# RWKV time mixing: six batches transposed on TensorE instead of by DMA transposes out of DRAM

## The chip, the cores and the metric

The kernel runs on one core of a Trainium2 chip. The metric is the device time of one execution in microseconds (us). Each kernel is run several times; one further execution is taken with the hardware profiler, and its durations are those quoted below. A core has TensorE (PE: matmuls and transposes; its weight loads are shown as PEld), VectorE (DVE), ScalarE (ACT), GpSimd (POOL), SyncE (SP, which here only issues transfers) and 16 DMA engines.

## The reference

x has 16 batches of 2048 tokens with 256 channels, float32. What counts for the output:

```python
x_prev[:, 1:, :] = x[:, :-1, :]          # the token before; zeros for the first
xv = x * time_mix_v + x_prev * (1 - time_mix_v)
xr = x * time_mix_r + x_prev * (1 - time_mix_r)
v = xv @ value_weight                    # 256 x 256
r = xr @ receptance_weight
out = (sigmoid(r) * v) @ output_weight
```

The key path of the reference does not reach its output, and the kernel leaves it out.

## The kernel before

**Units.** The 32768 tokens are cut into 64 units of 512 tokens (TU), four to a batch (UB). Channels lie on the partitions: 256 channels are two halves of 128 (KO), so x must be transposed before it can be mixed and multiplied. A batch is loaded by one software DMA from GpSimd (load, line 158 or 162), which also casts float32 to bf16.

**Two ways to a transposed x.** Batches 0 to 9 are loaded into SBUF tiles x_bf (four buffers), 16 tokens to a partition. For each of their units transposes() issues 8 transposes of 128x128 on TensorE into a PSUM tile ps_t (line 272), and ScalarE copies ps_t to xt_both (line 289). A slot of 128 columns then holds every 16th token, so the previous token of a slot is mostly the slot before it; one slot of a batch is a copy of another, shifted by one column (wrap_slots, line 557). Batches 10 to 15 (STAGED and up) are loaded into a DRAM tile x_natural as bf16 instead, in two groups of three, with 16 rows of zeros ahead of each batch (zero_rows, line 142). Two DMA transposes issued from SP (by_dma, line 254), in the passes of units 27 and 39 (T_AT), put a whole group into xt_both with tokens in their natural order. They wait for the loads of their group, and three later loads (STAGE_AT) wait for the first of them. Stores whose units are named in FIRST and WAITING are held back and issued around the DMA transposes.

**One unit.** With the mixing folded into the weights, a projection's input is c * previous + current. The product is made for one half of the channels on VectorE (line 354) and for the other on GpSimd (line 364), over two units at once from unit 10 on; VectorE adds the current tokens (line 376). project() (line 384) does four matmuls of 512 columns for r into psum_r and four for v into psum_v; ScalarE makes the sigmoid (line 658); VectorE multiplies it with psum_v into z_sb (line 697). output() multiplies z with the output weight in eight matmuls of 256 columns (line 416), ScalarE copies the result to an output tile (line 471), and SP stores it (line 437), two units to a store. Output tiles come from opool (seven buffers) and, late in the run, also from the x_bf buffers that are no longer needed.

**Order.** The order of each engine's instructions is the order in which the program writes them. The loop at the end of the kernel writes one pass for each unit g: r of unit g; the transposes of unit g + 6 (advance; LOOK is 6), with the loads that LOADS ties to them; v of unit g; z; the output of the unit before. In the free stage, from FREE = 34 on, when no transposes are left, ScalarE makes VectorE's product for v (scale_act, line 638), and the output runs two units behind instead of one.

Of the kernel before, what the change touches and what calls it, by code (L numbers as in the profile page):

```python
# [15 lines left out]
def kernel(  # L16
# [25 lines left out]
    nc = tc.nc  # L42
# [13 lines left out]
    STAGED = 10  # L56
    BYDMA = NU - STAGED * UB
    CROSS = NU - BYDMA - LOOK
    FREE = CROSS
    LATE_O = CROSS - 2  # L60
    T_AT = {27: 10, 39: 13}
    FIRST = {19: 27, 21: 27, 27: 39}
    WAITING = {23: 27, 25: 27, 29: 39, 31: 39, 33: 39, 35: 39}
    ZEROS_AT = 12
    SINGLE = NU - 6
    STAGED_PAIRS = range(STAGED, B - 1)
    STAGE_AT = {33: 13, 34: 14, 35: 15}
    GROUPS = [(2, 3), (4, 5, 6), (7, 8, 9), (10, 11, 12), (13, 14, 15)]
    HALVED = (12, 15)
    PAD = 16  # L70
    SPARE = 9 * UB // 2
# [7 lines left out]
    LOADS = {  # L79
        (1, 1): (3,),  # L80
        (1, 2): (4,),
        (2, 0): (5,),
        (3, 0): (6,),
        (4, 0): (7,),
        (5, 0): (8, 10),
        (6, 0): (9,),
        (7, 0): (11,),
        (7, 1): (12,),
    }
# [3 lines left out]
    dpool = ctx.enter_context(tc.tile_pool(name="dpool", bufs=2, space=bass.MemoryType.DRAM))  # L93
# [14 lines left out]
    kept = {}  # L108
    firsts = {}
    x_bf = {}  # L110
    x_both = {}
    loads = {}
# [20 lines left out]
    def new_staged(group):  # L133

        x_both[group[0]] = dpool.tile([len(group), PAD + S, D], BF16, name="x_natural")
        for k in range(len(group)):
            x_bf[group[0] + k] = x_both[group[0]][k, PAD:].rearrange("(p j) d -> p j d", p=P)
        return [(group[0], k) for k in range(len(group))]

    def zero_rows(b, k):  # L140
        rows = zeros[k * PAD : (k + 1) * PAD].rearrange("p (o c) -> p o c", o=1)
        nc.gpsimd.dma_start(
            out=x_both[b][k, :PAD].rearrange("p (h c) -> p h c", c=P),
            in_=rows.to_broadcast([PAD, KO, P]),
        )

    def load(b):
        if b < STAGED:
            x_bf[b] = xpool.tile([P, J, D], BF16, name="x_bf")
        if b < BYUNIT:  # L150
            for e in range(UB):
                nc.gpsimd.dma_start(  # L152
                    out=x_bf[b][:, e * UJ : (e + 1) * UJ, :], in_=unit_rows(x, b, e)[:, 0]
                )
            return
        if b in HALVED:
            return [
                nc.gpsimd.dma_start(out=x_bf[b][:, j : j + J // 2], in_=rows(b)[:, j : j + J // 2])
                for j in (0, J // 2)
            ]  # L160
        run = 8192 if b < LONG else 16384
        return nc.gpsimd.dma_start(out=x_bf[b], in_=rows(b), max_dma_last_dim=run)  # L162
# [47 lines left out]
    def new_xt(b):  # L210
        if b >= BYUNIT:
            for group in GROUPS:
                if b != group[0]:
                    continue
                if b >= STAGED:
                    t = xtpool.tile([P, KO, len(group) * (PAD + S)], BF16, name="xt_both")
                    for k in range(len(group)):
                        xt[b + k] = t[:, :, k * (PAD + S) + PAD - 1 : (k + 1) * (PAD + S)]
                    xt_both[b] = t
                    return  # L220
                xt_both[b] = xtpool.tile([P, J + 1, KO, len(group), P], BF16, name="xt_both")
                for k in range(len(group)):
                    xt[b + k] = xt_both[b][:, :, :, k]
                    nc.gpsimd.memset(xt[b + k][:, 0, :, 0:1], 0.0)
            return
        xt[b] = consts.tile([P, UB * (UJ + 1), KO, P], BF16, name=f"xt_first{b}")
        (nc.vector if b == 0 else nc.gpsimd).memset(xt[b][:, 0, :, 0:1], 0.0)
# [22 lines left out]

    def by_dma(b, after):

        new_xt(b)
        op = nc.sync.dma_start_transpose(
            out=xt_both[b], in_=x_both[b].rearrange("b s d -> (b s) d")
        )
        tc.add_manual_dep(op.ins, after.ins.name, SYNC, reason="not beside a load")
        return op
# [61 lines left out]
    def by_unit(cols, lo, hi):  # L320

        assert hi - lo in (TU, 2 * TU)
        return cols if hi - lo > TU else cols[:, :, :, lo // TU % 2]

    def tokens(piece, off, ko=None):

        b, _, lo, hi = piece
        if b in STAGED_PAIRS:
            pair = lo // (2 * TU) * 2 * TU + off
            cols = xt[b][:, :, pair : pair + 2 * TU].rearrange("p k (q h i) -> p k q h i", h=2, i=UJ)  # L330
            cols = by_unit(cols, lo, hi)
            return cols if ko is None else cols[:, ko]
        if b < STAGED:
            cols = xt[b][:, slots(piece, off)]
        else:
            cols = xt[b][:, :, off + lo : off + hi].rearrange("p k (j c) -> p j k c", c=P)
        return cols if ko is None else cols[:, :, ko]

    def mixed(piece, ko=None):
        b, m, lo, hi = piece  # L340
        cols = mix[(b * S + lo) // (2 * TU)][:, m]
        if b in STAGED_PAIRS:
            cols = cols.rearrange("p j k c -> p (j k c)")
            cols = cols.rearrange("p (h k q i) -> p k q h i", h=2, k=KO, i=UJ)
            cols = by_unit(cols, lo, hi)
            return cols if ko is None else cols[:, ko]
        j = lo // P % (2 * UJ)
        cols = cols[:, j : j + (hi - lo) // P]
        return cols if ko is None else cols[:, :, ko]
# [56 lines left out]
    def out_matmuls(ps, z, b, jj, n, whole=False):  # L406

        if whole:
            slot = z.rearrange("p k (c j) -> p k j c", j=UJ)[:, :, jj : jj + n]
        else:  # L410
            cols = z[:, :, jj * P : (jj + n) * P]
            order = "p k (j c) -> p k j c" if b < STAGED else "p k (c j) -> p k j c"
            slot = cols.rearrange(order, j=n)
# [10 lines left out]
    def store(queue, b, lo, hi, after=None):  # L424
        src = o_sb[b, lo // (2 * UJ)]
        j = lo % (2 * UJ)
        src = src[:, j : j + hi - lo, :]
        if b < STAGED:
            dst = out[b].rearrange("(p j) d -> p j d", p=P)[:, lo:hi, :]
        elif b in STAGED_PAIRS:  # L430
            h = lo // (2 * UJ)
            dst = out[b, h * 2 * TU : (h + 1) * 2 * TU].rearrange("(p j) d -> p j d", p=P)[:, j : j + hi - lo]
        else:
            n = min(hi - lo, UJ)
            dst = out[b, lo * P : hi * P].rearrange("(e p j) d -> p e j d", p=P, j=n)
            src = src.rearrange("p (e j) d -> p e j d", j=n)
        op = queue.dma_start(out=dst, in_=src)
        if after is not None:
            tc.add_manual_dep(op.ins, after.ins.name, SYNC, reason="in turn with the last load")

    def out_part(pool, name, z, b, e, jj, n, copy, queue):
        ps = pool.tile([P, n, D], FP32, name=name)
        out_matmuls(ps, z, b, jj, n)
# [5 lines left out]
    def new_o(b, h):  # L449

        n = b * UB // 2 + h - SPARE
        spare = n >= 0 and n % (NO + NX) < NX
        pool, name = (xpool, "x_bf") if spare else (opool, "o_sb")
        o_sb[b, h] = pool.tile([P, 2 * UJ, D], FP32, name=name)

    def output(g, z):
# [5 lines left out]
        if g >= NU - 4:  # L462
            for h in range(2):
                ps = ps_t_pool.tile([P, H, D], FP32, name="ps_t")
                out_matmuls(ps, z, b, h * H, H, whole=True)
# [4 lines left out]
        out_matmuls(ps, z, b, 0, UJ)  # L470
# [8 lines left out]
        elif e % 2 == 1:  # L479
            pair = (b, (e - 1) * UJ, (e + 1) * UJ)  # L480
            if g in FIRST:
                firsts.setdefault(FIRST[g], []).append(pair)
            elif g in WAITING:
                kept.setdefault(WAITING[g], []).append(pair)
            else:
                store(nc.sync, *pair)
# [76 lines left out]
    pads = [p for group in GROUPS if group[0] >= STAGED for p in new_staged(group)]  # L563
    tnext = 1

    def advance(limit):
        nonlocal tnext
        while tnext <= min(limit, NU - 1):
            b, e = divmod(tnext, UB)
            for n in LOADS.get((b, e), ()):  # L570
                loads[n] = load(n)
            if tnext < NU - BYDMA:
                transposes(tnext)
# [72 lines left out]
    for g in range(NU - 1):  # L646
# [13 lines left out]
        if g in T_AT:  # L660
            half, whole = loads[T_AT[g] + 2]
            for pair in firsts.pop(g):
                store(nc.sync, *pair, after=half)
            last_t = by_dma(T_AT[g], whole)
            for pair in kept.pop(g, []):
                store(nc.sync, *pair)
# [39 lines left out]
        if ZEROS_AT <= g < ZEROS_AT + len(pads):  # L706
            zero_rows(*pads[g - ZEROS_AT])
        if g in STAGE_AT:
            b = STAGE_AT[g]
            loads[b] = load(b)  # L710
            for op in loads[b] if b in HALVED else [loads[b]]:
                tc.add_manual_dep(op.ins, last_t.ins.name, SYNC, reason="not beside transposes")
# [36 lines left out]
```

## Time and profile before

| | |
|---|---|
| runs | 199.0, 202.78 and 715.19 us, median 202.78 |
| profiled execution | 198.87 us, its span 197.1 us |
| busy in the span | PE 191.5, DVE 183.1, ACT 177.1, POOL 86.3 us |
| transposes on TensorE (L272), bf16 | 304, the last at 111 us |
| copies out of ps_t (L289) | 38 of about 1.03 us |
| DMA transposes | 2, of 15.2 us (from 95.4) and 12.9 us (from 133.9) on SP's queue |
| bytes moved by DMA | 58.13 MB, 295 GB/s on average |

The span runs from the first to the last recorded event. A busy time is the sum of an engine's instructions in it. The chain of work that ended last is followed back from the last instruction to whatever released each one; with each step stands its engine, the tile that it writes and the line (L272 is line 272). Windows give the busy time of each engine in a stretch, with the number of instructions in brackets, then the granted clock of TensorE, the share of the DMA engines and GB/s. A row of the waits names the engine that waits and its line, what it waits for, the total in us, the number of times and the longest.

### The profile page before, as it was taken

The numbers are of one execution on the slowest core, as the hardware profiler recorded it, in microseconds if no ns is written. First come the engines' busy times: TensorE is split into PE (matmuls) and PEld (weight loads), VectorE is DVE, ScalarE is ACT, GpSimd is POOL, SyncE is SP. The second block draws the span as 40 slices with busy tenths as digits, with TensorE's granted clock in tenths as the row PEclk, the third lists the DMA queues.
The fourth block names the chain that finished last, engine by engine and source line by source line (L and its number), as shares of the span: only waits on it lengthen the run. The fifth ranks groups of instructions, "written<-read, shape, count | busy, mean of one in ns | idle before, by whom it ended". The sixth has DMA issues, their size and how long they took to land.

```text
span 197.1 us, 3735 instructions
## 1 busy us (share of the span) xinstructions
PE 191.5 (97%) x1358; PEld 123.0 (62%) x1364; DVE 183.1 (93%) x286; ACT 177.1 (90%) x197; POOL 86.3 (44%) x117
## 2 busy tenths in 40 slices
PE   8999999999999999999999999999999999999992
PEld 3556676666666666666666666666666666666660
DVE  0999999999999999999999999999999999999962
ACT  3699899999999999999999999999999999999982
POOL 2845542443665635624334266444433444444200
PEclk9999999999999999999999999999999999999998
DMA  5999999999999999999999999999999999999985
GB/s 185 238 176 224 218 254 262 247 259 262 296 413 283 283 296 332 283 238 198 376 209 290 335 346 186 212 218 241 290 290 419 419 421 419 416 416 421 382 327 221
DMA packets 35593, 58.13 MB, mean 295 GB/s; under 512 B 26004, under 2 KB 27128, under 8 KB 30840
## 3 DMA queue, kind: packets, MB, share of 16 engines
q1 hardware_dynamic: 31792, 41.34, 60.3%
q0 software_dynamic: 3632, 16.44, 41.6%
q8 instruction: 10, 0.16, 0.3%
q10 hardware_dynamic: 152, 0.13, 0.2%
q14 instruction: 7, 0.06, 0.1%
HBM read 34.34 MB, written 39.90 MB: 377 GB/s over the span
## 4 chain that ended last, share of the span: by engine, by line
PE 90%; DMA 6%; POOL 1%; issue 0%; SPq 0%; ACT 0%
PE psum_r L384 27%; PE psum_v L384 27%; PE psum_o L416 27%; PE ps_t L272 8%; DMA x_bf<-in_x_dram 4%; DMA w_f<-n_receptance_weight_dram 2%; PE ps_t L416 1%; POOL x_bf L192 1%; SPq L174 0%; POOL wo_bf L195 0%; PE psum_v L416 0%; POOL x_bf L152 0%; PE ps_t L384 0%; PE psum_r L416 0%; ACT x_bf L446 0%
## 5 line engine op out<-in xcount | busy, mean ns | idle before, releaser
L364 POOL TENSOR_SCALAR mix<-xt_both,c_sb 128x1024 bf16<-128x1024 bf16 (+1 forms) x55 | 61.1, 1110 | 85.5 <-DVE mix L376 82.3
L697 DVE TENSOR_TENSOR z_sb<-s_sb,psum_v 128x1024 bf16<-128x1024 bf16 (+1 forms) x64 | 76.8, 1201 | 2.3 <-PE psum_v L384 1.1
L376 DVE TENSOR_TENSOR mix<-mix,xt_both 128x1024 bf16<-128x1024 bf16 x112 | 76.8, 696 | 1.4
L384 PEld LDWEIGHTS <-w_bf 128*128 128x128 bf16 x512 | 48.5, 98 | 39.2 <-DVE mix L376 0.8
L658 ACT ACTIVATE s_sb<-psum_r 128x1024 bf16<-128x1024 f32 x63 | 65.2, 1034 | 6.2 <-PE psum_r L384 6.0
L384 PE MATMUL psum_v<-mix,w_bf 128*128 128x512 bf16 (+1 forms) x252 | 64.8, 378 | 0.4 <-DVE mix L376 0.2
L384 PE MATMUL psum_r<-mix,w_bf 128*128 128x512 bf16 x250 | 64.6, 379 | 0.2
L416 PE MATMUL psum_o<-wo_bf,z_sb 128*128 128x256 bf16 x486 | 63.2, 273 | 0.0
L416 PEld LDWEIGHTS <-z_sb 128*128 128x128 bf16 x512 | 52.0, 103 | 17.9 <-DVE z_sb L510 0.7
L471 ACT COPY o_sb<-psum_o 128x1024 f32<-128x1024 f32 x50 | 51.2, 1023 | 5.0 <-PE psum_o L416 4.8
L289 ACT COPY xt_both<-ps_t 128x1024 bf16<-128x1024 bf16 x32 | 32.9, 1039 | 0.0
L272 PEld LDWEIGHTS <-x_bf 128*128 128x128 bf16 x304 | 19.8, 98 | 8.4 <-DMA x_bf<-in_x_dram 0.4
L272 PE MATMUL ps_t<-ident,x_bf 128*128 128x128 bf16 x304 | 22.7, 219 | 0.2 <-DMA x_bf<-in_x_dram 0.2
L354 DVE TENSOR_SCALAR mix<-xt_both,c_sb 128x1024 bf16<-128x1024 bf16 (+1 forms) x47 | 21.3, 463 | 0.0
L638 ACT ACTIVATE mix<-xt_both,c_sb 128x1024 bf16<-128x1024 bf16 x14 | 16.3, 1163 | 0.0
L376 DVE TENSOR_TENSOR mix<-mix,xt_first 128x1024 bf16<-128x1024 bf16 x15 | 10.5, 708 | 0.1
L471 ACT COPY x_bf<-psum_o 128x1024 f32<-128x1024 f32 x10 | 10.2, 1015 | 0.0
L354 DVE TENSOR_SCALAR mix<-xt_first,c_sb 128x512 bf16<-128x512 bf16 x22 | 6.6, 350 | 0.3 <-ACT xt_first L282 0.2
L289 ACT COPY xt_first<-ps_t 128x1024 bf16<-128x1024 bf16 x6 | 6.0, 1022 | 0.0
L557 POOL COPY xt_first<-xt_first 128x254 bf16<-128x254 bf16 x5 | 2.0, 392 | 7.2 <-DVE mix L376 7.2
L162 POOL DMA_DIRECT2D x_bf<-in_x_dram x8 | 4.7, 584 | 0.0
L364 POOL TENSOR_SCALAR mix<-xt_first,c_sb 128x512 bf16<-128x512 bf16 x6 | 4.1, 685 | 1.3 <-DVE mix L376 0.8
(68 smaller groups left out, 52.3 us busy)
## 6 DMA issues: line engine op xcount, KB each, us to landing
out_dram<-o_sb SPq DMA_DIRECT2D x25, 1024.0 KB, 12.1
x_bf<-in_x_dram POOLq DMA_DIRECT2D x8, 1024.0 KB, 15.8
x_natural<-in_x_dram POOLq DMA_DIRECT2D x4, 1024.0 KB, 11.8
out_dram<-x_bf SPq DMA_DIRECT2D x4, 1024.0 KB, 14.4
x_natural<-in_x_dram POOLq DMA_DIRECT2D x4, 512.0 KB, 12.7
out_dram<-x_bf SPq DMA_DIRECT2D x4, 512.0 KB, 4.7
x_bf<-in_x_dram POOLq DMA_DIRECT2D x6, 256.0 KB, 7.0
o_sb<-in_x_dram SPq DMA_DIRECT2D x4, 256.0 KB, 3.9
```

Source lines behind the costliest of these rows:

```text
L162: return nc.gpsimd.dma_start(out=x_bf[b], in_=rows(b), max_dma_last_dim=run)
L272: nc.tensor.transpose(out=ps[:, jj], in_=src[:, jj, ko * P : (ko + 1) * P], identity=idn)
L289: nc.scalar.copy(out=xt[b][:, j0 : j0 + UJ], in_=ps)
L354: nc.vector.tensor_scalar(out=mixed(piece, ko), in0=tokens(piece, 0, ko), scalar1=c_sb[:, m, ko : ko + 1], scalar2=None, op0=ALU.mult,)
L364: op = nc.gpsimd.tensor_scalar(out=mixed(piece, 1), in0=tokens(piece, 0, 1), scalar1=c_sb[:, m, 1:2], scalar2=1.0, op0=ALU.mult, op1=ALU.mult,
L376: return nc.vector.tensor_tensor(out=mixed(piece), in0=mixed(piece), in1=tokens(piece, 1), op=ALU.add)
L384: nc.tensor.matmul(out=ps[:, mo, :], lhsT=w_bf[:, m, ko, mo * P : (mo + 1) * P], rhs=mixed((b, m, e * TU + lo, e * TU + hi), ko), start=(k ...
L416: nc.tensor.matmul(out=ps[:, j, :], lhsT=slot[:, ko, j], rhs=wo_bf[:, ko, :], start=(ko == 0), stop=(ko == KO - 1),)
L471: nc.scalar.copy(out=o[:, j0 : j0 + UJ, :], in_=ps)
L638: nc.scalar.activation(out=mixed(piece, ko), in_=tokens(piece, 0, ko), func=ACT.Copy, scale=c_sb[:, m, ko : ko + 1],)
L658: nc.scalar.activation(out=s_sb, in_=ps_r, func=ACT.Sigmoid)
L697: nc.vector.tensor_tensor(out=z_sb[:, :, c : c + n], in0=s_sb[:, :, c : c + n], in1=ps_v[:, :, c : c + n], op=ALU.mult,)
```

## The change

All batches take the way of batches 0 to 9. Batches 10 to 15 are loaded into x_bf, each with the transposes of the batch three ahead of it, and their 24 units are transposed on TensorE and copied out by ScalarE. The staging tiles in DRAM, the rows of zeros, the DMA transposes, the held stores and the second order of tokens are gone, and with them the special cases in tokens, mixed, out_matmuls and store. CROSS becomes 58 and with it FREE, so the free stage begins at unit 58; LATE_O becomes 56. Output tiles come from opool alone. From SINGLE = 54 on (before: 58) units are stored one by one.

```diff
-    STAGED = 10
-    BYDMA = NU - STAGED * UB
-    CROSS = NU - BYDMA - LOOK
+    CROSS = NU - LOOK
     FREE = CROSS
     LATE_O = CROSS - 2
-    T_AT = {27: 10, 39: 13}
-    FIRST = {19: 27, 21: 27, 27: 39}
-    WAITING = {23: 27, 25: 27, 29: 39, 31: 39, 33: 39, 35: 39}
-    ZEROS_AT = 12
-    SINGLE = NU - 6
-    STAGE_AT = {33: 13, 34: 14, 35: 15}
+    SINGLE = NU - 10
...
-        (5, 0): (8, 10),
-        (6, 0): (9,),
-        (7, 0): (11,),
-        (7, 1): (12,),
-    }
+    LOADS = {(1, 1): 3, (1, 2): 4, **{(b - 3, 0): b for b in range(5, B)}}
...
-        if b < STAGED:
-            x_bf[b] = xpool.tile([P, J, D], BF16, name="x_bf")
+        x_bf[b] = xpool.tile([P, J, D], BF16, name="x_bf")
...
-                if b >= STAGED:
-                    t = xtpool.tile([P, KO, len(group) * (PAD + S)], BF16, name="xt_both")
...
-    def by_dma(b, after):
-        new_xt(b)
-        op = nc.sync.dma_start_transpose(
-            out=xt_both[b], in_=x_both[b].rearrange("b s d -> (b s) d")
-        )
...
-        spare = n >= 0 and n % (NO + NX) < NX
-        pool, name = (xpool, "x_bf") if spare else (opool, "o_sb")
-        o_sb[b, h] = pool.tile([P, 2 * UJ, D], FP32, name=name)
+        o_sb[b, h] = opool.tile([P, 2 * UJ, D], FP32, name="o_sb")
...
-            pair = (b, (e - 1) * UJ, (e + 1) * UJ)
-            if g in FIRST:
-                firsts.setdefault(FIRST[g], []).append(pair)
-            elif g in WAITING:
-                kept.setdefault(WAITING[g], []).append(pair)
-            else:
-                store(nc.sync, *pair)
+            store(nc.sync, b, (e - 1) * UJ, (e + 1) * UJ)
...
-            for n in LOADS.get((b, e), ()):
-                loads[n] = load(n)
-            if tnext < NU - BYDMA:
-                transposes(tnext)
+            if (b, e) in LOADS:
+                load(LOADS[b, e])
+            transposes(tnext)
...
-        if g in T_AT:
-            half, whole = loads[T_AT[g] + 2]
-            for pair in firsts.pop(g):
-                store(nc.sync, *pair, after=half)
-            last_t = by_dma(T_AT[g], whole)
-            for pair in kept.pop(g, []):
-                store(nc.sync, *pair)
```

More of the change, by code (lines that the diff above doesn't have):

```diff
@@ L55 @@
     H = UJ // 2
-    STAGED = 10
-    BYDMA = NU - STAGED * UB
-    CROSS = NU - BYDMA - LOOK
+    CROSS = NU - LOOK
     FREE = CROSS
     LATE_O = CROSS - 2
-    T_AT = {27: 10, 39: 13}
-    FIRST = {19: 27, 21: 27, 27: 39}
-    WAITING = {23: 27, 25: 27, 29: 39, 31: 39, 33: 39, 35: 39}
-    ZEROS_AT = 12
-    SINGLE = NU - 6
-    STAGED_PAIRS = range(STAGED, B - 1)
-    STAGE_AT = {33: 13, 34: 14, 35: 15}
+    SINGLE = NU - 10
     GROUPS = [(2, 3), (4, 5, 6), (7, 8, 9), (10, 11, 12), (13, 14, 15)]
-    HALVED = (12, 15)
-    PAD = 16
-    SPARE = 9 * UB // 2
     NX, NO = 4, 7
@@ L78 @@
     SHIFT_ACT = (8,)
[L79 to L84, printed above, removed]
-        (5, 0): (8, 10),
-        (6, 0): (9,),
-        (7, 0): (11,),
-        (7, 1): (12,),
-    }
+    LOADS = {(1, 1): 3, (1, 2): 4, **{(b - 3, 0): b for b in range(5, B)}}
     consts = ctx.enter_context(tc.tile_pool(name="consts", bufs=1))
     xpool = ctx.enter_context(tc.tile_pool(name="xpool", bufs=NX))
-    dpool = ctx.enter_context(tc.tile_pool(name="dpool", bufs=2, space=bass.MemoryType.DRAM))
     xtpool = ctx.enter_context(tc.tile_pool(name="xtpool", bufs=2))
@@ L107 @@
     shifted = []
-    kept = {}
-    firsts = {}
     x_bf = {}
-    x_both = {}
-    loads = {}
     xt_both = {}
@@ L131, in unit_rows @@
         return t[b, e * TU : (e + n) * TU, :].rearrange("(e p j) d -> p e j d", p=P, j=UJ)
[L133 to L144, printed above, removed]
-        )
     def load(b):
-        if b < STAGED:
-            x_bf[b] = xpool.tile([P, J, D], BF16, name="x_bf")
+        x_bf[b] = xpool.tile([P, J, D], BF16, name="x_bf")
         if b < BYUNIT:
@@ L155, in load @@
             return
[L156 to L160, printed above, removed]
         run = 8192 if b < LONG else 16384
@@ L214, in new_xt @@
                     continue
-                if b >= STAGED:
-                    t = xtpool.tile([P, KO, len(group) * (PAD + S)], BF16, name="xt_both")
[L217 to L220, printed above, removed]
                 xt_both[b] = xtpool.tile([P, J + 1, KO, len(group), P], BF16, name="xt_both")
@@ L249, in coefficients @@
         nc.vector.tensor_scalar(out=c_sb, in0=c_sb, scalar1=-1.0, scalar2=None, op0=ALU.add)
-    def by_dma(b, after):
-        new_xt(b)
-        op = nc.sync.dma_start_transpose(
-            out=xt_both[b], in_=x_both[b].rearrange("b s d -> (b s) d")
-        )
-        tc.add_manual_dep(op.ins, after.ins.name, SYNC, reason="not beside a load")
-        return op
     def transposes(i):
@@ L318, in slots @@
         return slice(j, j + (hi - lo) // P)
-    def by_unit(cols, lo, hi):
-        assert hi - lo in (TU, 2 * TU)
-        return cols if hi - lo > TU else cols[:, :, :, lo // TU % 2]
     def tokens(piece, off, ko=None):
[L327 to L334, printed above, removed]
-        else:
-            cols = xt[b][:, :, off + lo : off + hi].rearrange("p k (j c) -> p j k c", c=P)
+        cols = xt[piece[0]][:, slots(piece, off)]
         return cols if ko is None else cols[:, :, ko]
@@ L341, in mixed @@
         cols = mix[(b * S + lo) // (2 * TU)][:, m]
[L342 to L346, printed above, removed]
         j = lo // P % (2 * UJ)
@@ L404, in project_unmixed, with out_matmuls @@
             )
[L406 to L413, printed above, removed]
+    def out_matmuls(ps, z, jj, n):
+        slot = z[:, :, jj * P : (jj + n) * P].rearrange("p k (j c) -> p k j c", j=n)
         for j in range(n):
@@ L422, in out_matmuls, with store @@
                 )
-    def store(queue, b, lo, hi, after=None):
-        src = o_sb[b, lo // (2 * UJ)]
+    def store(queue, b, lo, hi):
         j = lo % (2 * UJ)
[L427 to L439, printed above, removed]
+        queue.dma_start(
+            out=out[b].rearrange("(p j) d -> p j d", p=P)[:, lo:hi, :],
+            in_=o_sb[b, lo // (2 * UJ)][:, j : j + hi - lo, :],
+        )
     def out_part(pool, name, z, b, e, jj, n, copy, queue):
         ps = pool.tile([P, n, D], FP32, name=name)
-        out_matmuls(ps, z, b, jj, n)
+        out_matmuls(ps, z, jj, n)
         lo = e * UJ + jj
@@ L449, in new_o @@
     def new_o(b, h):
-        n = b * UB // 2 + h - SPARE
-        spare = n >= 0 and n % (NO + NX) < NX
-        pool, name = (xpool, "x_bf") if spare else (opool, "o_sb")
-        o_sb[b, h] = pool.tile([P, 2 * UJ, D], FP32, name=name)
+        o_sb[b, h] = opool.tile([P, 2 * UJ, D], FP32, name="o_sb")
     def output(g, z):
@@ L464, in output @@
                 ps = ps_t_pool.tile([P, H, D], FP32, name="ps_t")
-                out_matmuls(ps, z, b, h * H, H, whole=True)
+                out_matmuls(ps, z, h * H, H)
                 nc.scalar.copy(out=o[:, j0 + h * H : j0 + (h + 1) * H, :], in_=ps)
@@ L469, in output @@
         ps = ps_o_pool.tile([P, UJ, D], FP32, name="psum_o")
-        out_matmuls(ps, z, b, 0, UJ)
+        out_matmuls(ps, z, 0, UJ)
         nc.scalar.copy(out=o[:, j0 : j0 + UJ, :], in_=ps)
@@ L479, in output @@
         elif e % 2 == 1:
-            pair = (b, (e - 1) * UJ, (e + 1) * UJ)
-            if g in FIRST:
-                firsts.setdefault(FIRST[g], []).append(pair)
-            elif g in WAITING:
-                kept.setdefault(WAITING[g], []).append(pair)
-            else:
-                store(nc.sync, *pair)
+            store(nc.sync, b, (e - 1) * UJ, (e + 1) * UJ)
     def last_unit(g):
@@ L561, in wrap_slots @@
             tc.add_manual_dep(op.ins, after.ins.name, SYNC, reason="one at a time")
-    pads = [p for group in GROUPS if group[0] >= STAGED for p in new_staged(group)]
     tnext = 1
@@ L705 @@
             scale_pool(p, last)
[L706 to L712, printed above, removed]
         for p in held[g]:
```

## The prediction

> **What bounds the kernel now.** I read four views: the page, the chain of work that ended last, two long windows, and the waits in the second window. The page first:
>
> ```profile
> PE 191.5 (97%) x1358; PEld 123.0 (62%) x1364; DVE 183.1 (93%) x286; ACT 177.1 (90%) x197; POOL 86.3 (44%) x117
> ...
> PEclk9999999999999999999999999999999999999998
> ...
> PE 90%; DMA 6%; POOL 1%; issue 0%; SPq 0%; ACT 0%
> PE psum_r L384 27%; PE psum_v L384 27%; PE psum_o L416 27%; PE ps_t L272 8%; DMA x_bf<-in_x_dram 4%; DMA w_f<-n_receptance_weight_dram 2%; PE ps_t L416 1%; POOL x_bf L192 1%; SPq L174 0%; POOL wo_bf L195 0%; PE psum_v L416 0%; POOL x_bf L152 0%; PE ps_t L384 0%; PE psum_r L416 0%; ACT x_bf L446 0%
> ```
>
> TensorE is busy 97% of the span and is 90% of the last chain; its clock is granted in full throughout. But 97% is an average over two stages: transposes on TensorE (L272) end at 111 us. So I take the chain in order of time across that point. Columns are start, length, engine and step:
>
> ```profile
> 102.65 0.45 PE ps_t L272 x8
> 103.09 0.86 PE psum_v L384 x4
> 103.96 0.87 PE psum_o L416 x8
> 104.83 0.86 PE psum_r L384 x4
> 105.69 0.45 PE ps_t L272 x8
> ...
> 114.89 0.86 PE psum_v L384 x4
> 115.76 0.86 PE psum_r L384 x4
> 116.62 0.87 PE psum_o L416 x8
> 117.49 0.86 PE psum_v L384 x4
> ```
>
> Before the point a unit is four blocks on TensorE, 0.86 + 0.87 + 0.86 + 0.45 = 3.04 us, and the next ps_t starts 3.04 us after the last. Behind it a unit is three blocks, and psum_v recurs after 2.60 us. Nothing lies between the blocks in either stage. The two stages as windows, each cut from one start of psum_v to another; first column the window, then its length and the busy time of each engine:
>
> ```profile
> 39.12:109.19 70.07, 70.07 (x553) 46.25 (x552) 67.44 (x100) 65.80 (x71) 33.03 (x42) 1.00 1.05 286
> 112.25:185.09 72.84, 72.53 (x443) 45.68 (x448) 72.55 (x99) 67.25 (x71) 33.48 (x32) 1.00 1.06 342
> ```
>
> The z product (L697) is counted 23 times in the first and 28 times in the second, so the pitches are 70.07/23 = 3.046 and 72.84/28 = 2.601 us a unit. PE fills 100% and 99.6%. DVE fills 99.6% of the second as well: that stage stands on two legs. In it nobody waits for a transfer:
>
> ```profile
> POOL mix L364 <- DVE mix L376: 38.9, 27, 2.3
> ACT s_sb L658 <- PE psum_r L384: 5.6, 14, 0.5
> POOL mix L364 <- PE psum_v L384: 1.3, 1, 1.3
> PEld L416 <- issue: 0.2, 1, 0.2
> ```
>
> The DMA transposes that the change removes are thus hidden, and the three-block pitch exists because they are not on TensorE.
>
> **TensorE's part.** Batches 10 to 15 are 24 units; they get 8 transposes each, 192 in all (the changed program has 496 bf16 ones against 304). A unit's transposes are issued six units ahead, so those of units 40 to 63 stand in the passes of units 34 to 57: 24 passes grow from three blocks to four. A block of 8 is 0.445 us in the chain (0.45 and 0.44 alternate), so 24 x 0.445 = 10.7 us; by the pitches, 24 x (3.046 - 2.601) = 10.7 us as well. TensorE is the path there and has 0.3 us of slack in 73, so all of it shows. The mean of 219 ns in the row of L272 is a latency of overlapping instructions and is no price here (192 x 0.219 = 42 us).
>
> Here the Trainium skill speaks on both sides. TensorE: Matmul & The Clock Gate, Back-to-back issue gap, gives pairs of weight load and 128-column matmul a sustained spacing of about 81 ns; an estimate from that is 192 x 0.081 = 15.6 us, a time near 214.4. The chain shows the same pairs at 0.445/8 = 56 ns in this kernel, so I keep 10.7. VectorE: DVE Perf Modes, Rules for kernel authors, advises TensorE for a 128x128 transpose where PSUM is acceptable as its target, and The three transpose paths prices one at 390 ns there against 1309 ns by DMA; by these prices alone the change saves. The two DMA transposes take 15.2 and 12.9 us on SP's queue, but with no engine waiting the saving on the path is zero.
>
> **ScalarE.** 24 copies of transposed PSUM (L289, 1.02 us in the timeline) come in, 24.5 us. The free stage, in which ScalarE makes the first product of v (L638, 1.163 us, 14 of them), shrinks from pairs 36 to 62 to pairs 60 and 62, so 12 go: 14.0 us out. A unit is then as in the first window, 65.80/23 = 2.86 us of 3.046. It fits under TensorE; without that cover it would be 0.26 us a unit over the old pitch.
>
> **VectorE.** It takes back the 12 products (L354, 0.483 us): 5.8 us. Transposed batches need a shifted copy of the slot at their seam (L557, 0.218 us): 6 more, 1.3 us. Adds are 32.67/47 = 0.695 us in the first window and 37.37/56 = 0.667 in the second, so 48 of them gain 0.028 each, 1.3 us. Sum 8.4 over 24 units, 0.35; with 72.55/28 = 2.59 that is 2.94, and the first window shows 67.44/23 = 2.93. It fits under 3.046 with 0.11 us to spare. If the cover were gone, VectorE alone would hold the pitch at 2.93.
>
> **POOL and SP.** POOL loses six writes of zeros (0.55 us each) and eight staging loads (0.58), and issues six loads into SBUF (0.58): 4.5 us of issue less, and 6 small memsets (0.13 us) more on an engine that waits 83 us for VectorE; zero on the path. Each load now sits ahead of one POOL product, which comes 0.58 us later; its wait for VectorE before a product (34.5 us in 21 waits of the first window, 1.6 each) absorbs it, and eight loads of the first stage did this already. SP loses both transposes and the stores held behind them; it carries stores only. Zero.
>
> **Transfers.** The 6 batches no longer pass through DRAM: 6.3 MB written and 6.3 MB read back fall away. What is left per unit is 0.26 MB into SBUF and 0.52 MB out, 0.79 MB in 3.046 us, 258 GB/s in the profile's count. The window from 36 to 48 us runs at 256 with exactly this mix, slices of the first stage reach 332 and 413. A load has 12 units (36 us) between its issue and its first use, and lands 15.8 us after issue; its buffer was freed just before. Bounds: a late batch could cost some us, and less traffic could give up to 0.5 back at the end; I take zero, as the first window shows it.
>
> **Seams and tail.** The seam at 109 to 115 us costs nothing visible (units of 3.06, then 2.64), and now lies between units 57 and 58. Its place changes, not its price. In the tail the last copy starts at 193.39, and the final 128 KB stores land in 2.1 to 2.3 us. Four more single-unit stores replace pair stores near the end; between -0.5 and +0.5, taken as zero. The start is untouched.
>
> **Sum.** Span 197.1 + 10.7 = 207.8; 1.8 us lie around the span in the profiled execution (198.87), so 209.5 us. The runs shown are 199.0, 202.78 and 715.19; the profile agrees with the lowest, the median stands 3.9 above it. Against 198.87 the change is 5.4% slower, against 202.78 it is 3.3%. About 2% is what a measurement of this kernel can tell from no change.
>
> **Rivals.**
> Another engine or a transfer lengthens the four-block pitch. For: VectorE has only 0.11 us of slack a unit, the windows from 20 to 40 us show it full, and loads and stores now overlap to unit 57. Against: 23 units in succession at 3.046. Between 0.05 and 0.2 us a unit more, 1.2 to 4.8 us: 211 to 214. Chance 0.09.
> Not slower: the removed DRAM traffic pays for the transposes at the end. Place: the stores, which SP queued behind the transposes (one wait of 19.6 us for a staging load in the second window), then drain at about 416 GB/s from 147 to 185 us. If that queue set the end, its removal would shorten the tail. It decides from 6.7 us on (10.7 less 4.0, 2% of the time). Against: the whole tail behind the last copy's start is 3.7 us, and the last stores land in some 2 us each, so the queue is empty by then. With a 0.5 us gain it gives 209.0; to win it would have to end at 202.8 or below. Chance 0.03.
> Half of the transposes hide: if the second stage's PE blocks contained waiting that the modelled ends conceal, the transposes would fill it. Then VectorE's 2.93 would be the pitch: 24 x (2.93 - 2.60) = 7.9 us, 206.8. Against: the same blocks have the same 0.86 and 0.87 in both stages. Chance 0.04.
>
> **Numbers.** The forecast holds 0.84, centred on 209.5 with about 1 us either way. The range adds part of both slower-pitch cases and a slightly disturbed median, 207.6 to 212.5. Slower by over 2% in all cases but the tail's: 0.96; within 2% 0.03; faster 0.01.
>
> **What would show it.** Right: 496 bf16 transposes, one block of 0.445 us in each pass to unit 57, a pitch of 3.04 to 3.05 from 39 us to about 182, PE at 100% there, ScalarE near 94% and VectorE near 96%, no wait for in_x_dram behind 16 us, pitch 2.60 in the last units alone, span near 207.8. Wrong: gaps between TensorE's blocks with VectorE or an x_bf load as releaser; a granted clock under 1.00 in that stretch; or a pitch under 3.0 with four blocks in it.

## The result and the profile after

The changed kernel takes 210.06 us (median of four runs, 209.81 to 210.51); the ratio to the kernel before is 1.0549, 95% interval 1.051 to 1.0587. The ratio is taken to the undisturbed runs of the kernel before, 199.0 and 199.36 us; its slow ones of 202.78 and 715.19 us are left out. The change makes the kernel 10.9 us slower, about the 10.7 us of the forecast. The profiled execution has 209.86 us and a span of 208.0.

The page of the changed kernel, the lines that answer to those of before (here L211 is the transposes, L304 the projections, L330 the output matmuls):

```profile
PE 202.2 (97%) x1556; PEld 131.5 (63%) x1556; DVE 190.3 (92%) x304; ACT 187.9 (90%) x209; POOL 81.9 (39%) x115
...
PE 92%; DMA 4%; SPq 0%; POOL 0%; issue 0%; ACT 0%
PE psum_v L304 26%; PE psum_r L304 26%; PE psum_o L330 26%; PE ps_t L211 13%; DMA x_bf<-in_x_dram 2%; DMA w_f<-n_receptance_weight_dram 2%; PE ps_t L330 1%; SPq L128 0%; POOL x_bf L146 0%; PE psum_v L330 0%; PE ps_t L304 0%; PE psum_r L330 0%; ACT o_sb L350 0%
...
L211 PE MATMUL ps_t<-ident,x_bf 128*128 128x128 bf16 x496 | 37.2, 220 | 0.2 <-DMA x_bf<-in_x_dram 0.2
```

TensorE's share of the span is 97% in both kernels. The transposes went from 8% to 13% of the chain, from 304 to 496 instructions, and the three other blocks keep their 26 or 27% each. The chain in order of time, across the place where the kernel before went over to three blocks, and then across its new place (start, length, engine and step):

```profile
111.76 0.45 PE ps_t L211 x8
112.20 0.86 PE psum_v L304 x4
113.07 0.87 PE psum_o L330 x8
113.94 0.86 PE psum_r L304 x4
114.80 0.45 PE ps_t L211 x8
...
182.28 0.86 PE psum_v L304 x4
...
184.02 0.45 PE ps_t L211 x8
...
185.34 0.86 PE psum_v L304 x4
...
187.98 0.86 PE psum_v L304 x4
```

A unit stays at four blocks and 3.04 us to the v that starts at 182.28; one more block of transposes follows at 184.02, and then a unit takes 2.64 us. The long window of the changed kernel, from one start of psum_v to another (window, length, busy PE, PEld, DVE, ACT, POOL, clock, DMA share, GB/s), and its waits:

```profile
39.08:182.28 143.20, 143.20 (x1130) 94.51 (x1128) 136.98 (x202) 134.10 (x143) 57.82 (x68) 1.00 0.87 264
```

```profile
POOL mix L284 <- DVE mix L296: 80.2, 45, 2.3
ACT o_sb L372 <- PE psum_o L330: 9.1, 45, 0.2
POOL mix L284 <- ACT xt_both L228: 4.6, 2, 2.7
DVE z_sb L583 <- PE psum_v L304: 2.4, 9, 0.6
```

The window holds 47 z products, so the pitch is 143.20/47 = 3.047 us, the 3.046 of the first stage before. TensorE has no gap in it. The four rows are all the waits there are: the others wait for TensorE or for each other, and nobody for a transfer.

The whole difference of the two spans can be placed. From the start of psum_v at 109 us (109.19 before, 109.16 after) to the start of the last copy (193.39 and 204.08) the kernel before takes 84.20 us and the changed one 94.92: 10.72 more. What lies ahead gives back 0.03, the tail behind the last copy grows from 3.7 to 3.9. Together 10.9, which is 208.0 - 197.1. (The kernel with late loads, further down, stores as the changed one does and has a tail of 3.7, so these 0.2 us may be scatter.) What was spared outside TensorE is real but worth nothing there: the bytes moved fall from 58.13 to 51.77 MB, a load of a batch into SBUF lands after 12.1 us in the median of 14 (15.8 before, in the median of 8), a store of two units after 8.5 (12.1).

### The profile page after: what moved, and what is told of

Read it like the earlier page. It is cut to its first block, busy times and chain, and to the rows that moved or that the text cites. A ratio compares the mean times of both kernels' runs of the same rounds, so it can differ in the third digit from the quotient of the medians.

```text
span 208.0 us, 4156 instructions
## 1 busy us (share of the span) xinstructions
PE 202.2 (97%) x1556; PEld 131.5 (63%) x1556; DVE 190.3 (92%) x304; ACT 187.9 (90%) x209; POOL 81.9 (39%) x115
## 2 busy tenths in 40 slices
DMA packets 10571, 51.77 MB, mean 249 GB/s; under 512 B 1076, under 2 KB 2104, under 8 KB 5816
## 4 chain that ended last, share of the span: by engine, by line
PE 92%; DMA 4%; SPq 0%; POOL 0%; issue 0%; ACT 0%
PE psum_v L304 26%; PE psum_r L304 26%; PE psum_o L330 26%; PE ps_t L211 13%; DMA x_bf<-in_x_dram 2%; DMA w_f<-n_receptance_weight_dram 2%; PE ps_t L330 1%; SPq L128 0%; POOL x_bf L146 0%; PE psum_v L330 0%; PE ps_t L304 0%; PE psum_r L330 0%; ACT o_sb L350 0%
## 5 line engine op out<-in xcount | busy, mean ns | idle before, releaser
L296 DVE TENSOR_TENSOR mix<-mix,xt_both 128x1024 bf16<-128x1024 bf16 x112 | 78.1, 699 | 2.6
L372 ACT COPY o_sb<-psum_o 128x1024 f32<-128x1024 f32 x60 | 61.3, 1022 | 9.8 <-PE psum_o L330 9.8
L304 PEld LDWEIGHTS <-w_bf 128*128 128x128 bf16 x512 | 47.4, 98 | 33.7 <-DVE mix L296 0.4
L304 PE MATMUL psum_v<-mix,w_bf 128*128 128x512 bf16 (+1 forms) x256 | 65.3, 378 | 0.0
L304 PE MATMUL psum_r<-mix,w_bf 128*128 128x512 bf16 x252 | 64.7, 379 | 0.0
L330 PE MATMUL psum_o<-wo_bf,z_sb 128*128 128x256 bf16 x486 | 63.2, 273 | 0.0
L330 PEld LDWEIGHTS <-z_sb 128*128 128x128 bf16 x512 | 49.8, 98 | 19.8 <-DVE z_sb L405 0.7
L228 ACT COPY xt_both<-ps_t 128x1024 bf16<-128x1024 bf16 x56 | 57.4, 1032 | 0.0
L211 PEld LDWEIGHTS <-x_bf 128*128 128x128 bf16 x496 | 32.4, 98 | 14.2 <-DMA x_bf<-in_x_dram 1.0
L211 PE MATMUL ps_t<-ident,x_bf 128*128 128x128 bf16 x496 | 37.2, 220 | 0.2 <-DMA x_bf<-in_x_dram 0.2
L274 DVE TENSOR_SCALAR mix<-xt_both,c_sb 128x1024 bf16<-128x1024 bf16 (+1 forms) x59 | 27.0, 465 | 0.0
L116 POOL DMA_DIRECT2D x_bf<-in_x_dram x14 | 8.1, 580 | 0.0
L158 PE MATMUL ps_t<-const-bfloat16-1.0 128*128 128x512 bf16 (+1 forms) x11 | 3.4, 465 | 0.8 <-PEq L612 0.8
## 6 DMA issues: line engine op xcount, KB each, us to landing
x_bf<-in_x_dram POOLq DMA_DIRECT2D x14, 1024.0 KB, 12.1
```

The costliest lines, as they stand in the source:

```text
L158: nc.tensor.matmul(out=ps[:, :cols], lhsT=ones, rhs=wide[:, :cols], start=True, stop=True)
L211: nc.tensor.transpose(out=ps[:, jj], in_=src[:, jj, ko * P : (ko + 1) * P], identity=idn)
L228: nc.scalar.copy(out=xt[b][:, j0 : j0 + UJ], in_=ps)
L274: nc.vector.tensor_scalar(out=mixed(piece, ko), in0=tokens(piece, 0, ko), scalar1=c_sb[:, m, ko : ko + 1], scalar2=None, op0=ALU.mult,)
L296: return nc.vector.tensor_tensor(out=mixed(piece), in0=mixed(piece), in1=tokens(piece, 1), op=ALU.add)
L304: nc.tensor.matmul(out=ps[:, mo, :], lhsT=w_bf[:, m, ko, mo * P : (mo + 1) * P], rhs=mixed((b, m, e * TU + lo, e * TU + hi), ko), start=(k ...
```

## The experiments

Theory A, that of the forecast: each engine needs a fixed time for a unit, the largest sets the pitch; TensorE's transposes are the whole price, and VectorE stands next behind it at 2.93 us, ScalarE at 2.86. The rivals are named in the expectations. The engines' own lines of code have other numbers in each kernel; operation and tile tell them apart. Each time quoted as a result is the median.

**The transposes alone, in the kernel before.** Nothing is taken away from it; TensorE gets eight more transposes in 24 passes, whose result nobody reads.

```diff
         advance(START_T[g] if g < len(START_T) else g + LOOK)
+        if 34 <= g < 58:
+            ps = ps_t_pool.tile([P, UJ, KO, P], BF16, name="ps_t")
+            for jj in range(UJ):
+                for ko in range(KO):
+                    c = jj % 2 * P
+                    nc.tensor.transpose(
+                        out=ps[:, jj, ko], in_=wo_bf[:, ko, c : c + P], identity=ident
+                    )
```

> The kernel before, with all its DMA transposes, staging and the early free stage, plus eight transposes of the output weight in each of the passes of units 34 to 57, whose result nobody reads. Theory A: TensorE's 192 transposes are the whole price of the change: 198.9 + 10.7 = 209.6, the same as the changed kernel within 1 us, pitch 3.046. Rival C (the removed DRAM traffic and DMA transposes gave something back in the changed kernel): slower than the changed kernel by what they are worth, 1 to 3 us, 211 to 213. Rival D (the price is the copies on ScalarE and the products on VectorE): near 199, since neither gets more work.

Measured: 209.94 us, beside 200.52 for the kernel before, timed with it; ratio 1.048 (1.0407 to 1.0552). The changed kernel has 210.06, theory A said 209.6. The chain of this kernel (L665 is the added transposes):

```profile
128.30 0.45 PE ps_t L665 x8
128.75 0.87 PE psum_o L416 x8
129.62 0.86 PE psum_v L384 x4
130.49 0.86 PE psum_r L384 x4
131.35 0.45 PE ps_t L665 x8
```

Rival D falls: neither ScalarE nor VectorE got any more work here, and the loss is the same. Rival C falls too: with staging, DMA transposes and DRAM traffic all still there, the time is that of the kernel without them. The medians alone tell this to about 1.5 us, since this kernel is 9.4 above the kernel before and the changed one 10.9. The traces tell it closer. From the start of the sigmoid of unit 10 (41.84 us before, 43.98 here, 41.80 in the changed kernel) to the start of ScalarE's last copy (193.39, 206.20, 204.08) the profiled executions take 151.55, 162.22 and 162.27 us. So the transposes alone cost 10.67 us, and all the rest of the change 0.05 between these points. (The profiled execution of this kernel took 211.72 us in all; its first sigmoid starts at 11.39 us, where it was 9.11 before and 9.22 in the changed kernel.)

**Half of the change.** Only batches 13 to 15 stay staged.

```diff
-    STAGED = 10
+    STAGED = 13
...
-    T_AT = {27: 10, 39: 13}
-    FIRST = {19: 27, 21: 27, 27: 39}
-    WAITING = {23: 27, 25: 27, 29: 39, 31: 39, 33: 39, 35: 39}
+    T_AT = {39: 13}
+    FIRST = {31: 39}
+    WAITING = {33: 39, 35: 39}
...
-    STAGE_AT = {33: 13, 34: 14, 35: 15}
+    STAGE_AT = {}
...
-    HALVED = (12, 15)
+    HALVED = (15,)
...
-    SPARE = 9 * UB // 2
+    SPARE = 12 * UB // 2
...
-        (5, 0): (8, 10),
+        (5, 0): (8,),
         (6, 0): (9,),
-        (7, 0): (11,),
-        (7, 1): (12,),
+        (7, 0): (10,),
+        (8, 0): (11, 13),
+        (9, 0): (12, 14),
+        (10, 0): (15,),
```

> Half of the change: the kernel before with only batches 13 to 15 staged in DRAM and transposed by DMA, and batches 10 to 12 loaded into SBUF and transposed on TensorE (12 units, passes 34 to 45). Theory A: 198.9 + 12 x 0.445 = 204.2. Rival C: if the first of the two DMA transposes disturbed something, less than half of the loss, 202 to 203. If the second needs the first's place in the order, more.

Measured: 205.2 us, ratio 1.0255 (1.0196 to 1.0313). It is 1.0 above the sum from 198.87, and 4.7 above the 200.52 of the kernel before, timed with it, where 12 units are worth 5.3. Between the two points named above its trace takes 157.24 us, 5.7 more than before: 5.34 for the 12 units and 0.33 for one unit just behind the stage (unit 48 takes 2.70 us; before, unit 36 at the same place took 2.37). Half of the loss comes with half of the units. The kernel is slower, though the interval does not rule out a loss just under 2%.

**Twice the transposes.** In the changed kernel each transpose of batches 10 to 15 is made twice.

```diff
-        for jj in range(UJ):
-            for ko in range(KO):
-                one(ps[:, :, ko], jj, ko, src, ident)
+        for _ in range(2 if b >= 10 else 1):
+            for jj in range(UJ):
+                for ko in range(KO):
+                    one(ps[:, :, ko], jj, ko, src, ident)
```

> The changed kernel with each transpose of batches 10 to 15 made twice into the same place, sixteen in each of 24 units. Theory A: TensorE is the path there and another 24 x 0.445 = 10.7 us come on top: about 220.6, pitch 3.49. By the rule of about 81 ns for such a pair it would be 15.6 more, about 225.5. Rival D (ScalarE or VectorE set the pitch): under 215.

Measured: 220.5 us (the median of two runs), 10.4 above the changed kernel's 210.06, 54 ns for each of the 192 more. The chain of this kernel (in it L305 is the projections, L331 the output):

```profile
128.99 0.89 PE ps_t L211 x16
129.88 0.86 PE psum_v L305 x4
130.74 0.87 PE psum_o L331 x8
131.62 0.86 PE psum_r L305 x4
132.48 0.89 PE ps_t L211 x16
```

Sixteen take 0.89 us, the unit 3.49. The price is linear in the transposes (0.45 us for eight, and 0.11 for two in the chain of the kernel with half adds below), at 56 ns each on the path. The sustained spacing of about 81 ns that the Trainium skill gives (TensorE: Matmul & The Clock Gate, Back-to-back issue gap), from which the estimate of 225.5 comes, does not hold here. Rival D is out once more.

**What stands behind TensorE.** In the changed kernel six of the eight transposes of each of the 24 units are left out, and ScalarE's copy reads the two that are made four times over.

```diff
+        few = b >= 10
-        for jj in range(UJ):
+        for jj in range(1 if few else UJ):
             for ko in range(KO):
                 one(ps[:, :, ko], jj, ko, src, ident)
-        nc.scalar.copy(out=xt[b][:, j0 : j0 + UJ], in_=ps)
+        got = ps[:, 0:1].to_broadcast([P, UJ, KO, P]) if few else ps
+        nc.scalar.copy(out=xt[b][:, j0 : j0 + UJ], in_=got)
```

> In the changed kernel, the 24 units of batches 10 to 15 get two of their eight transposes; ScalarE copies those two slots four times over, so its copy has the full 1024 columns (the input of these units is wrong by that). TensorE then needs 2.60 + 2 x 0.056 = 2.71 us a unit. Theory A (each engine needs what its busy time in the first stage shows, the largest sets the pitch): VectorE takes over at 2.93, so the 24 units win only 24 x (3.046 - 2.93) = 2.8 us: about 207.1 us, VectorE at 99% and gaps between TensorE's blocks. Rival B (only TensorE's work counts, the busy time of VectorE is elastic): 24 x 6 x 0.056 = 8.0 us less, about 201.9 us, no gaps.

Measured: 207.21 us, where A said 207.1 and B 201.9. The sigmoids of 14 units start between 135.44 and 176.46 us, so the pitch is 41.02/14 = 2.93. The chain of this kernel has left TensorE in that stretch:

```profile
133.79 0.39 issue
134.18 1.21 DVE z_sb L585
135.38 0.62 DVE mix L298
136.01 0.14 DVE xt_both L454
136.14 0.41 DVE mix L276
```

It runs along VectorE's own instructions: z, an add, the shifted copy of a seam, a product (the 0.39 us called issue lie under an add that VectorE makes from 133.57 to 134.25). Without 75% of the transposes' work only a quarter of their price is won back, since VectorE and ScalarE carry the changed kernel's other work. From 120 to 180 us ScalarE was 97% busy beside VectorE's 98%, so this run alone does not tell which of the two it was. The 2.93 is met better than its working deserves: over the 14 units VectorE is busy 40.29 us, 2.88 a unit, and the rest of the pitch is idle time.

**Relieve VectorE as well.** On top of that, VectorE adds the current tokens for half of the slots only.

```diff
+        n = UJ // 2 if b >= 10 else UJ
         return nc.vector.tensor_tensor(
-            out=mixed(piece), in0=mixed(piece), in1=tokens(piece, 1), op=ALU.add
+            out=mixed(piece)[:, :n], in0=mixed(piece)[:, :n], in1=tokens(piece, 1)[:, :n], op=ALU.add
         )
```

> The kernel with two of eight transposes (207.2 us), and VectorE's adds of batches 10 to 15 over half of the slots only (the input of these units is wrong by both). VectorE then needs some 0.65 us a unit less, about 2.28. Theory A1 (VectorE was the next bound at 2.93, ScalarE follows at its 2.86): 24 x 0.07 = 1.7 us less, about 205.5, ScalarE at 99%. Theory A2 (ScalarE was the bound): no change, 207.2. Rival B (only TensorE's 2.71 counts once VectorE is out of the way): about 201.9.

Measured: 203.78 us. VectorE was the bound (A2 falls). ScalarE does follow it, as A1 says, but at 2.75 us and not at 2.86. From 127 to about 156 us the chain is TensorE's, three blocks and two transposes, and psum_r recurs after 2.71 us:

```profile
131.28 0.86 PE psum_r L307 x4
132.15 0.11 PE ps_t L211 x2
...
133.99 0.86 PE psum_r L307 x4
```

From 157 to 177 us the chain runs along ScalarE's copies and sigmoids, which follow each other without a gap. The window from 145 to 177 us, and ScalarE's instructions in it:

```profile
145.00:177.00 32.00, 31.84 (x208) 19.42 (x206) 27.83 (x51) 32.00 (x37) 12.53 (x16) 1.00 0.59 235
```

```profile
159.40 1.35 ACT L554 ACTIVATE s_sb<-psum_r 128x1024 bf16<-128x1024 f32 x1
160.32 1.34 ACT L230 COPY xt_both<-ps_t 128x1024 bf16<-128x1024 bf16 x1
161.25 1.33 ACT L375 COPY o_sb<-psum_o 128x1024 f32<-128x1024 f32 x1
162.16 1.35 ACT L554 ACTIVATE s_sb<-psum_r 128x1024 bf16<-128x1024 f32 x1
```

From sigmoid to sigmoid three of them take 2.75 us, so that is what ScalarE needs for a unit. The 2.86 of the first stage was a busy time, not a need: in the timeline of before, too, ScalarE's instructions start about 0.91 us apart when they follow each other, though each lasts 1.02, since each record begins before the one ahead of it ends. A unit with one gap in it has two such overlaps and a longer busy time than a unit without a gap, which has three. The whole run lies 1.9 us above rival B: about 0.7 of it in the units 37 to 40, which still take 2.8 to 3.1 us (the transposes run six units ahead, so the adds are whole ones until about 130 us), 0.3 in later ones of 2.75, and about 1.0 where the stage ends (units 57 to 60 take 10.77 us, in the changed kernel 10.44).

**Relieve ScalarE too, with GpSimd's help.** ScalarE copies two slots, GpSimd copies them on to the other two.

```diff
-        got = ps[:, 0:1].to_broadcast([P, UJ, KO, P]) if few else ps
-        nc.scalar.copy(out=xt[b][:, j0 : j0 + UJ], in_=got)
+        n = UJ // 2 if few else UJ
+        got = ps[:, 0:1].to_broadcast([P, n, KO, P]) if few else ps
+        nc.scalar.copy(out=xt[b][:, j0 : j0 + n], in_=got)
+        if few:
+            nc.gpsimd.tensor_copy(out=xt[b][:, j0 + n : j0 + UJ], in_=xt[b][:, j0 : j0 + n])
```

> As the kernel with half adds, and ScalarE copies only two slots of ps_t in these 24 units (0.43 us less, about 2.43 a unit); GpSimd, idle for most of the stage, copies them to the other two. Theory A: now TensorE's 2.71 is the largest, 24 x (3.046 - 2.71) = 8.0 us under the changed kernel: about 201.9, TensorE without gaps. If GpSimd's copy delays its products: between 202 and 207.

Measured: 206.95 us, slower than without the relief, at the upper end of what was allowed for a late product. From 120 to 180 us ScalarE has time to spare (busy 49.6 of the 60), and VectorE is the path again (busy 59.0), though it has no instruction more. The group of its half adds from 140 to 176 us, first without and then with GpSimd's copies (engine, operation, tiles, shape and count, then busy us, mean ns and idle time):

```profile
L299 DVE TENSOR_TENSOR mix<-mix,xt_both 128x512 bf16<-128x512 bf16 x27 | 11.3, 420 | 0.7
```

```profile
L302 DVE TENSOR_TENSOR mix<-mix,xt_both 128x512 bf16<-128x512 bf16 x26 | 17.3, 665 | 0.6
```

The same add takes 665 ns on average instead of 420. The last section shows where this comes from.

**The loads.** Batches 10 to 15 are loaded one batch ahead of their transposes, no longer three.

```diff
-    LOADS = {(1, 1): 3, (1, 2): 4, **{(b - 3, 0): b for b in range(5, B)}}
+    LOADS = {(1, 1): 3, (1, 2): 4, **{(b - (3 if b < 10 else 1), 0): b for b in range(5, B)}}
```

> The changed kernel with the loads of batches 10 to 15 issued one batch ahead instead of three: 4 units, 12.2 us, before their first transpose, where a load landed after 12.1 us in the changed kernel's median. Theory A (loads are hidden with three batches to spare): the margin is used up here and a few batches come late; between 0 and 2 us for each of six, 210 to 216, with waits of L211 for in_x_dram. If loads set the pitch anywhere before, much more; if a load lands faster with fewer others beside it, 210.

Measured: 210.03 us, with no wait for in_x_dram in the stage. The six loads land after 8.7 to 11.2 us, median 9.5, inside the 12.2. The 12.1 of the expectation is the median over all 14 loads of the changed kernel; its seven from 60 us on landed after 9.4 in the median, so the margin was larger than it looked. Transfers do not touch the path even with a third of the lead.

**Single stores at the end.**

```diff
-    SINGLE = NU - 10
+    SINGLE = NU - 6
```

> The changed kernel with single-unit stores from unit 58 on, as before the change, instead of 54. The forecast took this part at zero, within 0.5 us: 209.9, the tail behind the last copy near 3.9 us as in the changed kernel.

Measured: 211.22 us (210.34 to 212.34), beside 210.03 for the kernel with late loads on the same chip. Three of its six runs lie at 210.3 to 210.6 and three at 211.9 to 212.3; the profiled one has a tail of 4.3 us, against 3.9 in the changed kernel and 3.7 in the one with late loads. Between the sigmoid of unit 10 and the last copy it takes 162.26 us, as they do (162.27 and 162.26). Inconclusive: pair stores to unit 58 are not better, and may cost some 1 us. Whether the four additional single stores of the change saved that is not settled.

None of these kernels is faster than the kernel before.

## Why the prediction was right, point by point

- **TensorE's part, 10.7 us.** Right in amount and place: 10.72 us between the same two points of the traces, transposes in blocks of 0.45 us, four blocks a unit up to the v of 182 us, as forecast. The transposes alone in the old kernel cost the same, half of the units about half, double the transposes double.
- **What was removed is worth zero.** Right: the old kernel with added transposes takes the same time, to 0.05 us between the two points of the traces.
- **VectorE, 2.93.** Right that VectorE stands next, and near 2.93: with TensorE relieved the pitch is 2.93. That both agree to two decimals is in part luck, for VectorE's busy time there is 2.88 a unit. The rival in which half of the transposes hide would have met this floor, but its condition, waiting inside TensorE's blocks, did not hold: sixteen transposes cost twice what eight do.
- **ScalarE.** The forecast of its busy share (94%) came true, 134.10 of 143.20. The clause that it would cost 0.26 us a unit without its cover is wrong: it took the busy time of 2.86 for a need. With VectorE relieved too, ScalarE held the pitch at 2.75, which is 0.15 over the old pitch. As TensorE covered it, the sum was not touched.
- **POOL, SP and the transfers, zero.** Right; no wait for a load in the stage, and a third of the lead was enough.
- **Seams and tail.** The seam cost nothing new (psum_v at 182.28, 185.34 and 187.98: 3.06 and 2.64, as before). The tail is 0.2 us longer, inside the half microsecond allowed and perhaps scatter.
- **Not slower.** It would have needed 6.7 us from the tail, which had 3.7.
- **The sum.** 209.5 against 210.06 measured and 209.86 in the profiled execution: the span grew by 10.9 us instead of 10.7, of which the tail is 0.2, and 1.9 lie outside it instead of 1.8.

## What to carry to other kernels

A step on the engine that sets the pitch costs its spacing in the chain, not its mean duration (here 56 ns, not 220) and not the price of the operation it replaces; a slower engine that is off the path is the cheaper place. A neighbouring stage with the same blocks gives the pitch of a stage that will look like it: 3.046 us was read there, 3.047 came out. The busy time of the engines behind the first one is only an upper bound of what they need, where their records overlap.

## What the runs showed of the hardware that was not expected

VectorE's add of two bf16 operands in SBUF waits for GpSimd when it begins under one of GpSimd's instructions. In the timeline of the kernel with GpSimd's copies:

```profile
116.72 1.11 POOL L289 TENSOR_SCALAR mix<-xt_both,c_sb 128x1024 bf16<-128x1024 bf16 x1
...
116.87 1.50 DVE L302 TENSOR_TENSOR mix<-mix,xt_both 128x1024 bf16<-128x1024 bf16 x1
...
132.56 1.11 POOL L289 TENSOR_SCALAR mix<-xt_both,c_sb 128x1024 bf16<-128x1024 bf16 x1
...
133.16 0.78 DVE L302 TENSOR_TENSOR mix<-mix,xt_both 128x512 bf16<-128x512 bf16 x1
...
134.26 0.41 DVE L302 TENSOR_TENSOR mix<-mix,xt_both 128x512 bf16<-128x512 bf16 x1
```

GpSimd's second product ends at 133.67 and the half add that began under it at 133.94; the half add at 134.26 began under none. In the stage up to 180 us, 18 half adds began under a GpSimd product: all ended 0.27 to 0.28 us after it and lasted 0.78 to 1.18. The 18 that began under none lasted 0.41 to 0.43, also when a GpSimd instruction began during them. A whole add ends twice as long after the product, 0.54 us (118.37 and 117.83 above; and so in 23 of 23 cases in the kernel with two of eight transposes). So what is left behind the end looks like the add's own pass over its data, which has not begun before. The z product, with one operand in PSUM, lasts 1.21 us whether it begins under a GpSimd instruction (8 times) or not (15 times).

This agrees with the Trainium skill, SBUF — State Buffer, SBUF: two separate sides: the two engines share one pair of ports, which a VectorE operation needs when both its inputs lie in SBUF (against a GpSimd instruction that reads SBUF), and the later one waits for the whole instruction. The 0.27 and 0.54 us are these traces'.

In the kernel before and the changed one GpSimd's product starts about when VectorE's z does (131.62 and 131.46 us in the changed kernel) and lies nearly all under it, and the adds stay at 0.70 us on average. GpSimd's idle time is therefore not free to be filled. The copies did not hold up the half adds themselves, for none of these began under a copy; they pushed the product out from under z (the copy before the product of 132.56 runs from 131.84 to 132.58). The 18 adds held up last 16.5 us together, 18 free ones 7.5. Without GpSimd's copies VectorE had 6.9 us to spare in the 60 us from 120 (busy 53.1), so an estimate from these numbers is some 2 us of the 3.2 us that the kernel lost. That the adds, and not something else that the copies move, made the time was argued from these records and not tried apart.
